# Moving side work of a two-layer S5, retention and convolution trunk: sums at other gate blocks, k0 ahead of the last state-space output, low parts among the value products, one operand place fewer

## The chip, the cores and the metric

The kernel runs on one core of a Trainium2 chip. The metric is the device time of one execution in microseconds (us). Engine names are those of the profile: PE is TensorE (matmuls), PEld its weight loads, DVE is VectorE, ACT is ScalarE, POOL is GpSimd, SP is SyncE, which here issues every DMA from one queue in order (SPq).

## What is computed

A trunk of two layers on x of shape (1, 1024, 1024), each `x = x + mixer(rmsnorm(x))`, then a final norm. Layer 0's mixer, cut to what matters here:

```python
u_s5, g_s5, q, k, v, g_ret = jnp.split(h @ w_in, cuts, axis=-1)
y_s5 = s5_mixer(u_s5, ...)            # diagonal state space, gelu, GLU
y_s5 = y_s5 * jax.nn.silu(g_s5)
y_ret = retention(q, k, v) * jax.nn.silu(g_ret)   # 8 heads, rotary q and k
return jnp.concatenate([y_s5, y_ret], axis=-1) @ w_out
```

Layer 1 is a convolution module: an input projection into a, b and a gate, a width-31 depthwise convolution, a layer norm and an output projection.

## The kernel before, in words

Matrices lie transposed: features on the 128 partitions, the 1024 tokens in two halves of 512. Every large product is done with operands split into a high part and a low part (`wh`, `wl` for weights, `xh`, `xl` for x), and three matmuls per block of 128 (high x high, high x low, low x high; L269 to L271, `mm3`). A `gemm` is 24 matmuls of 128x512 for one half, so a projection block of 128 features takes 48. Weights come by DMA as `wf` (512 KB), ACT casts the high part `wh`, and DVE or POOL subtracts to get the low part `wl`. `wnext` hands them out in the order that `plan` laid down.

`layer0_front` makes x's parts, then blocks u0 to u7 (input of the state-space layer), then gate blocks g8 to g23, 48 matmuls each. Between the gate blocks stand the steps of the state-space layer for B = 0 to 7, two gate blocks each: `s5_tables` (POOL), `s5_states`, and `s5_out(B - 1)`. `s5_states` writes a kernel Kt to DRAM (`k_d`, L876), reads it back as a banded tile `Wd` (L879), and ACT copies it to `W1` (L881). `s5_out` runs 16 matmuls of W1 and U (L896) and 32 of W3 and S (L902) into two banks y0 and y1, ACT copies these to `yb` (L906), and a DMA stores `yb` in `y_d` (L908). `s5_out(7)` comes last, behind g23.

Three helpers make sums for Strassen-Winograd products and put them in DRAM, and are called inside the loop over the gate blocks, on tiles with the tags wa to wd, two of each. `input_sums` (4 calls) loads four quarters of x (256 KB each), scales and adds on ACT and DVE, and stores four sums `xt1` to `xt4`. `weight_sums` (8 calls) does the same for the output weights on DVE (`a`, `ws`, L237 to L247); `value_sums` (4 calls, POOL) for the value weights (`va`, `vs`). The calls for x stand behind gate blocks 9, 11, 13 and 15, those for the output weights behind blocks 16 to 23.

`retention` works by four pairs of heads. For each pair `ret_proj` projects k and q (48 matmuls each), DVE takes them out of PSUM as `kraw` and `qraw` (L970), four DMAs swap their halves (`kswp`, `qswp`, L979), POOL multiplies by the rotary tables (L983, L985) and DVE adds (`krot`, `qrot`, L986). In pair 0 `ret_values` follows: the value projection as seven products of half size (order 1, 2, 6, 7, 3, 4, 5; 48 matmuls each), whose x operands are four tile pairs each. Products 1, 2 and 3 use quarters of x itself; 6, 7, 4 and 5 use the sums xt2, xt3, xt4 and xt1, which `fetch` loads and splits into two places of 8 tiles. DVE and ACT then add the products and scale them per token into `v` (L1019). `ret_heads` transposes k (`ktp`, L1062), decays it (`kt`, L1064), makes state updates (`kv`, L1081; `S`, L1091), scores (`sp`, L1098; `sc`, L1104) and outputs (`ro`, L1125 and L1130), normalises them and multiplies by the gate. Each pair also makes two `y_pass` steps for the state-space branch: a load of `yp` from `y_d` (L915), gelu on ACT (`yn`, L917, with a table load), and a store to `yn_d` (L918).

`weight_low` prepares low parts of layer 1's input weights: a load `lf` of 256 KB (L224), a cast `lh` on ACT (L225), a subtraction on DVE (L226), a store `lo` (L229). `LOWS` = 16 of 32 are made in pairs 1 and 2, behind the second mask of that pair, on tiles with one buffer each; the rest in the GLU loop of `layer0_back_and_layer1`.

The order on each engine is set by a scheduler from the program's order, its own estimates of times, the pools' free buffers, and `issue_after`, which keeps what stands inside it from being issued before a named instruction. Each engine then runs its list in order. PSUM has 3 banks for projections (`ps_mm`) and 5 for the rest (`ps_aux`).

Of the kernel before, what the change touches and what calls it, by code (L numbers as in the profile page):

```python
# [19 lines left out]
P = 128  # L20
# [3 lines left out]
HALF = 512  # L24
# [32 lines left out]
class Trunk:  # L57
# [272 lines left out]
    def layer0_front(self, st):  # L330
# [3 lines left out]
        early = ExitStack()  # L334
# [585 lines left out]
    def retention(self, st):  # L920
        nc, A = self.nc, self.A
        r0 = self.r0 = self.pool("ret0", 1, stack=st)
        early = ExitStack()
        rq = self.rq = self.pool("retq", 1, stack=early, side="right")
        self.vt = [[(r0 if d else rq).tile([P, 4, HALF], F32, name=f"v{d}_{h}") for h in range(2)] for d in range(2)]
        self.rk = rq.tile([P, 2, T], F32, name="ropek")
        nc.sync.dma_start(self.rk[:], A["rope_k"])
        self.mask = r0.tile([P, NH, P], F32, name="retmask")
        nc.sync.dma_start(self.mask[:], A["ret_mask"])
        self.g128 = r0.tile([P, 4], F32, name="g128")  # L930
        nc.sync.dma_start(self.g128[:], A["ret_g128"])
        self.reps = r0.tile([P, NH], F32, name="reteps")
        nc.sync.dma_start(self.reps[:], A["ret_eps"])
        for pair in range(4):
            cur = list(self.ret_proj(pair))[-1]
            if pair == 0:
                with ExitStack() as vst:
                    V = self.ret_values(self.pool("vp", 1, stack=vst))
                self.rp = self.pool("ret", 1, stack=st)
                self.kdec = self.rp.tile([P, NH, 64], F32, name="kdec")  # L940
                nc.sync.dma_start(self.kdec[:], A["ret_kdec"])
                ry = self.pool("rety", 1, stack=early, side="right")
            with ExitStack() as held:
                if pair:
                    held.enter_context(self.tc.issue_after(self.last_rs.ins))
                for cb in (2 * pair, 2 * pair + 1):
                    self.y_pass(ry, cb)

            def turned():
                if pair == 3:  # L950
                    early.close()
                    self.lp = self.pool("l1", side="right")
            if pair in (1, 2):
                with self.tc.issue_after(self.masked[1].ins):
                    for k in range(LOWS // 2 * (pair - 1), LOWS // 2 * pair):
                        self.weight_low(ry, k, (("wa", "wb"), ("wc", "wd")), 1)
            self.ret_heads(pair, *cur, V, turned)

    def ret_proj(self, pair):
        nc, A, rp = self.nc, self.A, self.r0  # L960
        raws = {}

        def project(nm):
            w = self.wnext(f"{nm}{pair}")
            raw = raws[nm] = self.rq.tile([P, T], F32, name=f"{nm}raw_{pair}", tag="raw", bufs=2)
            for h in range(2):
                c = slice(h * HALF, (h + 1) * HALF)
                ps = self.bank(f"mm_{nm}{pair}_{h}", aux=False)
                self.gemm(ps[:], w, self.xs[h])
                last = nc.vector.tensor_tensor(raw[:, c], ps[:], self.R[:, c], op=ALU.mult)  # L970
            return last

        def turn(nm, behind=None):
            raw, tab = raws[nm], self.rk
            swp = self.rq.tile([P, T], F32, name=f"{nm}swp_{pair}", tag="swp", bufs=2)
            o = rp.tile([P, T], F32, name=f"{nm}rot_{pair}", tag=f"{nm}rot", bufs=1)
            for b in range(4):
                s = b ^ 1
                nc.sync.dma_start(swp[32 * b:32 * b + 32, :], raw[32 * s:32 * s + 32, :])  # L979
            cs = [slice(h * HALF, (h + 1) * HALF) for h in range(2)]  # L980

            for c in cs:
                nc.gpsimd.tensor_tensor(o[:, c], raw[:, c], tab[:, 0, c], op=ALU.mult)  # L983
            for c in cs:
                nc.gpsimd.tensor_tensor(swp[:, c], swp[:, c], tab[:, 1, c], op=ALU.mult)  # L985
            return o, [lambda c=c: nc.vector.tensor_tensor(o[:, c], o[:, c], swp[:, c], op=ALU.add) for c in cs]  # L986


        project("k")
        yield None  # L990
        krot, adds = turn("k")
        last = project("q")
        with self.tc.issue_after(last.ins):
            for add in adds:
                add()
        qrot, qadds = turn("q")
        if pair % 2 == 0:
            for add in qadds:
                add()
            qadds = ()  # L1000
        yield krot, qrot, qadds

    def ret_values(self, vp):
# [1 line left out]
        nc, v = self.nc, self.nc.vector  # L1005
        vt = self.vt

        def fetch(i, slot):
            res = []
            for kb in range(4):  # L1010
                a, b = (vp.tile([P, HALF], F32R, name=f"xt{i}{q}{kb}", tag=f"xt{slot}", bufs=8) for q in "hl")
                nc.sync.dma_start(b[:].bitcast(F32), self.xt_d[i][kb])
                nc.scalar.copy(a[:], b[:].bitcast(F32))
                v.tensor_tensor(b[:], b[:].bitcast(F32), a[:].bitcast(F32), op=ALU.subtract)
                res.append((a, b))
            return res
# [4 lines left out]
        xs = {1: self.xs[0][:4], 2: self.xs[0][4:], 3: self.xs[1][4:]}  # L1021
        m, u3 = ([vp.tile([P, HALF], F32, name=f"{n}{b}") for b in range(4)] for n in ("vm", "vu"))
        for n, i in enumerate(V_ORDER):
            if i in (1, 2):
                xs[i + 5] = fetch((2, 3)[i - 1], i)
            pss = [self.bank(f"mm_v{i}_{b}", aux=n % 2 == 0 or b == 3) for b in range(4)]
            for j in range(2):
                wh, wl = (t[:].rearrange("p (k a) n -> p k (a n)", a=4) for t in self.wnext(f"V{i}_{j}"))
                for b in range(4):
                    o = slice(b * P, (b + 1) * P)  # L1030
                    for k in range(2):
                        xh, xl = xs[i][2 * j + k]
                        first, last = j == k == 0, j == k == 1
                        nc.tensor.matmul(pss[b][:], xh[:, o], wh[:, k, :], start=first, stop=False)  # L1034
                        nc.tensor.matmul(pss[b][:], xh[:, o], wl[:, k, :], start=False, stop=False)  # L1035
                        nc.tensor.matmul(pss[b][:], xl[:, o], wh[:, k, :], start=False, stop=last)  # L1036
            if i in (6, 7):
                xs[{6: 4, 7: 5}[i]] = fetch({6: 4, 7: 1}[i], i - 5)
            for b, ps in enumerate(pss):
                if i == 1:  # L1040
                    nc.scalar.copy(m[b][:], ps[:])
                elif i in (2, 4):
                    v.tensor_tensor(ps[:], ps[:], (m if i == 2 else u3)[b][:], op=ALU.add)
                    scaled(i // 4, 0, b, ps[:])
                else:
                    v.tensor_tensor((u3 if i == 7 else m)[b][:], ps[:], m[b][:], op=ALU.add)
                    if i == 5:
                        scaled(0, 1, b, m[b][:])
                        v.tensor_tensor(ps[:], ps[:], u3[b][:], op=ALU.add)
                        scaled(1, 1, b, ps[:])  # L1050
# [686 lines left out]
```

## Time and profile before

| | us |
|---|---|
| median of 3 runs | 1213.87 (1213.17 to 1214.84) |
| the profiled execution | 1213.96 |
| its span | 1212.2 |
| outside the span | 1.8 |
| mean granted TensorE clock | 0.989 |

The profile is of one execution on the one core. Busy time counts an engine's instructions, not its waits. A timeline row gives the start in us from the span's start, the time, the engine, the line, the operation with the tiles it writes and reads, the shapes, and the number of instructions joined; behind it in brackets stands how long the engine had been idle and what ended that. A clock of 1.00 is TensorE's full speed. The DMA share is the mean busy share of the core's 16 DMA engines.

### The profile page before, as it was taken

The numbers are of one execution on the slowest core, as the hardware profiler recorded it, in microseconds if no ns is written. First come the engines' busy times: TensorE is split into PE (matmuls) and PEld (weight loads), VectorE is DVE, ScalarE is ACT, GpSimd is POOL, SyncE is SP. The second block draws the span as 40 slices with busy tenths as digits, with TensorE's granted clock in tenths as the row PEclk, the third lists the DMA queues.
The fourth block names the chain that finished last, engine by engine and source line by source line (L and its number), as shares of the span: only waits on it lengthen the run. The fifth ranks groups of instructions, "written<-read, shape, count | busy, mean of one in ns | idle before, by whom it ended". The sixth has DMA issues, their size and how long they took to land.

```text
span 1212.2 us, 17495 instructions
## 1 busy us (share of the span) xinstructions
PE 1173.8 (97%) x6150; PEld 972.0 (80%) x6150; DVE 920.3 (76%) x1525; ACT 550.4 (45%) x827; POOL 681.7 (56%) x489
## 2 busy tenths in 40 slices
PE   8999999999979999799899999999999999999997
PEld 7888888888868888678688888878887888788877
DVE  6966866899436537688788979469999999999643
ACT  7222333332124354234444645267765668444662
POOL 2059987788813233423344132518896578987642
PEclk9999999999989999899999999999999999999999
DMA  9362556587797546875898657865547653356863
GB/s 334 105 200 81 195 203 215 195 284 278 261 354 254 166 147 212 282 246 189 333 333 291 223 208 241 286 254 198 174 148 267 248 190 117 126 187 230 276 245 138
DMA packets 130904, 270.14 MB, mean 223 GB/s; under 512 B 12800, under 2 KB 41728, under 8 KB 130688
## 3 DMA queue, kind: packets, MB, share of 16 engines
q1 hardware_dynamic: 130816, 269.02, 65.2%
q8 instruction: 48, 0.79, 0.3%
q14 instruction: 40, 0.33, 0.1%
HBM read 193.02 MB, written 71.76 MB: 218 GB/s over the span
## 4 chain that ended last, share of the span: by engine, by line
PE 77%; DMA 8%; DVE 7%; POOL 2%; issue 2%; ACT 2%; SPq 1%; DVEq 0%; POOLq 0%; ACTq 0%
PE mm_g L271 6%; PE mm_g L270 6%; PE mm_g L269 6%; PE mm_w L269 4%; PE mm_w L270 4%; PE mm_w L271 3%; PE mm_u L271 2%; PE mm_u L270 2%; PE mm_oc L271 2%; PE mm_oc L269 2%; PE mm_oc L270 2%; PE mm_u L269 2%; PE mm_v L1036 2%; PE mm_v L1034 2%; PE mm_v L1035 2%
## 5 line engine op out<-in xcount | busy, mean ns | idle before, releaser
L1426 DVE SCALAR_TENSOR_TENSOR cv<-u,convw,cv 128x512 f32<-128x512 f32 x358 | 245.3, 748 | 5.7 <-ACT cv L1412 3.9
L1406 POOL TENSOR_TENSOR tp<-tp,tp 128x512 f32<-128x512 f32 x104 | 138.9, 1339 | 33.0 <-ACT tp L1405 27.3
L271 PE MATMUL mm_g<-xh,wl_g 128*128 128x512 f32 x256 | 100.8, 394 | 0.0
L270 PE MATMUL mm_g<-xl,wh_g 128*128 128x512 f32 x256 | 100.6, 393 | 0.0
L269 PE MATMUL mm_g<-xh,wh_g 128*128 128x512 f32 x256 | 100.4, 392 | 0.0
L1405 ACT ACTIVATE tp<-u,convw 128x512 f32<-128x512 f32 x104 | 69.3, 714 | 9.2 <-POOL tp L1406 9.0
L270 PEld LDWEIGHTS mm_g<-xl,wh_g 128*128 128x128 f32 x256 | 48.1, 188 | 11.3 <-issue 1.6
L271 PEld LDWEIGHTS mm_g<-xh,wl_g 128*128 128x128 f32 x256 | 48.0, 188 | 10.5
L269 PEld LDWEIGHTS mm_g<-xh,wh_g 128*128 128x128 f32 x256 | 48.1, 188 | 9.6
L271 PE MATMUL mm_oc<-zh,wl_woc 128*128 128x512 f32 (+1 forms) x152 | 54.7, 360 | 0.7 <-DMA wl_woc<-lo_woc 0.7
L269 PE MATMUL mm_oc<-zh,wh_woc 128*128 128x512 f32 (+1 forms) x152 | 54.5, 362 | 0.0
L270 PE MATMUL mm_oc<-zl,wh_woc 128*128 128x512 f32 (+1 forms) x152 | 54.2, 356 | 0.0
L271 PE MATMUL mm_g<-h1h,wl_cg 128*128 128x512 f32 x128 | 50.0, 390 | 1.1 <-POOL wl_cg L261 1.1
L270 PE MATMUL mm_u<-xl,wh_u 128*128 128x512 f32 x128 | 49.9, 390 | 0.9 <-DVE xl L383 0.9
L270 PE MATMUL mm_b<-h1l,wh_cb 128*128 128x512 f32 x128 | 50.5, 394 | 0.3 <-DVE h1l L1343 0.3
L270 PE MATMUL mm_glu<-yl,wh_glu 128*128 128x512 f32 x128 | 50.5, 395 | 0.2 <-DVE yl L1165 0.2
L269 PE MATMUL mm_glu<-yh,wh_glu 128*128 128x512 f32 x128 | 50.6, 397 | 0.0
L269 PE MATMUL mm_u<-xh,wh_u 128*128 128x512 f32 x128 | 49.4, 396 | 1.2 <-ACT wh_u L260 1.1
L271 PE MATMUL mm_glu<-yh,wl_glu 128*128 128x512 f32 x128 | 50.4, 394 | 0.0
L269 PE MATMUL mm_g<-h1h,wh_cg 128*128 128x512 f32 x128 | 50.3, 393 | 0.0
L271 PE MATMUL mm_a<-h1h,wl_ca 128*128 128x512 f32 x128 | 50.3, 393 | 0.0
L269 PE MATMUL mm_b<-h1h,wh_cb 128*128 128x512 f32 x128 | 49.9, 390 | 0.4 <-ACT h1h L1342 0.4
(833 smaller groups left out, 3607.7 us busy)
## 6 DMA issues: line engine op xcount, KB each, us to landing
wf_g<-w_ab SPq DMA_DIRECT2D x16, 512.0 KB, 4.6
a<-w_out SPq DMA_DIRECT2D x32, 256.0 KB, 4.5
ws<-a SPq DMA_DIRECT2D x32, 256.0 KB, 4.9
lf<-w_c SPq DMA_DIRECT2D x32, 256.0 KB, 5.1
wf_p<-ws SPq DMA_DIRECT2D x16, 512.0 KB, 3.8
wf_cb<-w_c SPq DMA_DIRECT2D x16, 512.0 KB, 4.8
wf_ca<-w_c SPq DMA_DIRECT2D x16, 512.0 KB, 4.8
wl_cb<-lo_cb SPq DMA_DIRECT2D x16, 512.0 KB, 3.4
```

What stands on the lines that cost most here:

```text
L269: nc.tensor.matmul(ps, wh[:, kb, :], xh, start=start, stop=False)
L270: nc.tensor.matmul(ps, wh[:, kb, :], xl, start=False, stop=False)
L271: self.last_mm = nc.tensor.matmul(ps, wl[:, kb, :], xh, start=False, stop=stop)
L1034: nc.tensor.matmul(pss[b][:], xh[:, o], wh[:, k, :], start=first, stop=False)
L1035: nc.tensor.matmul(pss[b][:], xh[:, o], wl[:, k, :], start=False, stop=False)
L1036: nc.tensor.matmul(pss[b][:], xl[:, o], wh[:, k, :], start=False, stop=last)
L1405: nc.scalar.mul(sk[:], u[:, k:k + HALF], cw[:, nb, k:k + 1])
L1406: gp.tensor_tensor(s0[:], s0[:], sk[:], op=ALU.add)
L1426: v.scalar_tensor_tensor(dst[:], *tap, accs_[i][:], op0=ALU.mult, op1=ALU.add)
```

## The change

1. `LOWS` goes from 16 to 18.
2. The calls of `input_sums` stand behind gate blocks 9, 10, 11 and 12, those of `weight_sums` behind 13 to 20.
3. k0's two gemms are issued at the end of `layer0_front`, ahead of `s5_out(7)`; their banks are kept, and `ret_proj` takes them from there.
4. The calls of `weight_low` leave pairs 1 and 2. `ret_values` makes three behind the last sum of each product from the second on, on the tags wa to wd with two buffers.
5. `ret_values` has one operand place of 8 tiles fewer. xt2 and later xt4 are split into the four tile pairs of x's first quarter of the second token half (`x12`), which no product reads; during product 5 that quarter is loaded again from `xT`, scaled and split. Loads go through staging tiles `xf` on the tags wa and wc.
6. The sums of the products are regrouped: product 1 and the sums of 7 and 3 are scaled on ACT as they come; 2, 4 and 5 are added with one scalar_tensor_tensor per target on DVE.

```diff
-LOWS = 16
+LOWS = 18
...
-                if nb >= 16:
-                    self.weight_sums(sums, nb - 16)
-                elif nb % 2:
-                    self.input_sums(sums, (nb - 8) // 2)
+                if 9 <= nb < 13:
+                    self.input_sums(sums, nb - 9)
+                elif 13 <= nb < 21:
+                    self.weight_sums(sums, nb - 13)
+        w, self.k0 = self.wnext("k0"), [self.bank(f"mm_k0_{h}", aux=False) for h in range(2)]
+        for h in range(2):
+            self.gemm(self.k0[h][:], w, xs[h])
         self.s5_out(7)
...
-            if pair in (1, 2):
-                with self.tc.issue_after(self.masked[1].ins):
-                    for k in range(LOWS // 2 * (pair - 1), LOWS // 2 * pair):
-                        self.weight_low(ry, k, (("wa", "wb"), ("wc", "wd")), 1)
...
-                ps = self.bank(f"mm_{nm}{pair}_{h}", aux=False)
-                self.gemm(ps[:], w, self.xs[h])
+                ps = self.k0[h] if early else self.bank(f"mm_{nm}{pair}_{h}", aux=False)
+                if not early:
+                    self.gemm(ps[:], w, self.xs[h])
...
+        def fetch(i, tiles):
+            for kb, (a, b) in enumerate(tiles):
+                g = self.vec(V_NG0, kb)
+                f = vp.tile([P, HALF], F32, name=f"xf{i}{kb}", tag=("wa", "wc")[kb % 2], bufs=2)
+                nc.sync.dma_start(f[:], self.xt_d[i][kb] if i else self.A["xT"][kb, :, HALF:])
+                if i:
+                    nc.scalar.copy(a[:], f[:])
+                    v.tensor_tensor(b[:], f[:], a[:].bitcast(F32), op=ALU.subtract)
+                else:
+                    nc.scalar.mul(a[:], f[:], g)
+                    v.scalar_tensor_tensor(b[:], f[:], g, a[:].bitcast(F32), op0=ALU.mult, op1=ALU.subtract)
+            return tiles
...
+        def summed(d, h, b, ps):
+            o, r = vt[d][h][:, b, :], self.Rtok[:, 4 * h + b:4 * h + b + 1]
+            self.last_sum = v.scalar_tensor_tensor(o, ps, r, o, op0=ALU.mult, op1=ALU.add)
+
+        x12 = self.xs[1][:4]
+        spare = [tuple(vp.tile([P, HALF], F32R, name=f"xt{q}{kb}") for q in "hl") for kb in range(4)]
+        xs = {1: self.xs[0][:4], 2: self.xs[0][4:], 3: self.xs[1][4:], 6: fetch(2, x12), 7: fetch(3, spare)}
...
             if i in (6, 7):
-                xs[{6: 4, 7: 5}[i]] = fetch({6: 4, 7: 1}[i], i - 5)
+                xs[{6: 4, 7: 5}[i]] = fetch(*{6: (4, x12), 7: (1, spare)}[i])
+            if i == 4:
+                fetch(0, x12)
             for b, ps in enumerate(pss):
                 if i == 1:
                     nc.scalar.copy(m[b][:], ps[:])
+                    scaled(0, 0, b, ps[:])
                 elif i in (2, 4):
-                    v.tensor_tensor(ps[:], ps[:], (m if i == 2 else u3)[b][:], op=ALU.add)
-                    scaled(i // 4, 0, b, ps[:])
+                    summed(i // 4, 0, b, ps[:])
+                elif i == 5:
+                    summed(0, 1, b, ps[:])
+                    summed(1, 1, b, ps[:])
                 else:
...
+                    t = (u3 if i == 7 else m)[b]
+                    self.last_sum = v.tensor_tensor(t[:], ps[:], m[b][:], op=ALU.add)
+                    for d, h in {6: (), 7: ((1, 0), (1, 1)), 3: ((0, 1),)}[i]:
+                        scaled(d, h, b, t[:])
+            with self.tc.issue_after(self.last_sum.ins) if n > 1 else nullcontext():
+                for k in range(LOWS * (n - 1) // 6, LOWS * n // 6) if n else ():
+                    self.weight_low(vp, k, (("wa", "wb"), ("wc", "wd")), 2)
```

More of the change, by code (lines that the diff above doesn't have):

```diff
@@ L963, in project @@
         def project(nm):
-            w = self.wnext(f"{nm}{pair}")
+            early = nm == "k" and pair == 0
+            w = None if early else self.wnext(f"{nm}{pair}")
             raw = raws[nm] = self.rq.tile([P, T], F32, name=f"{nm}raw_{pair}", tag="raw", bufs=2)
@@ L1006, in ret_values @@
         vt = self.vt
[L1008 to L1016, printed above, removed]
+        def fetch(i, tiles):
[10 more added lines that the diff above has]
+            return tiles
         def scaled(d, h, b, src):
             nc.scalar.mul(vt[d][h][:, b, :], src, self.Rtok[:, 4 * h + b:4 * h + b + 1])
-        xs = {1: self.xs[0][:4], 2: self.xs[0][4:], 3: self.xs[1][4:]}
+        def summed(d, h, b, ps):
[4 more added lines that the diff above has]
+        xs = {1: self.xs[0][:4], 2: self.xs[0][4:], 3: self.xs[1][4:], 6: fetch(2, x12), 7: fetch(3, spare)}
         m, u3 = ([vp.tile([P, HALF], F32, name=f"{n}{b}") for b in range(4)] for n in ("vm", "vu"))
         for n, i in enumerate(V_ORDER):
-            if i in (1, 2):
-                xs[i + 5] = fetch((2, 3)[i - 1], i)
             pss = [self.bank(f"mm_v{i}_{b}", aux=n % 2 == 0 or b == 3) for b in range(4)]
@@ L1041, in ret_values @@
                     nc.scalar.copy(m[b][:], ps[:])
+                    scaled(0, 0, b, ps[:])
                 elif i in (2, 4):
-                    v.tensor_tensor(ps[:], ps[:], (m if i == 2 else u3)[b][:], op=ALU.add)
-                    scaled(i // 4, 0, b, ps[:])
-                else:
[L1046 to L1050, printed above, removed]
+                    summed(i // 4, 0, b, ps[:])
+                elif i == 5:
+                    summed(0, 1, b, ps[:])
+                    summed(1, 1, b, ps[:])
+                else:
+                    t = (u3 if i == 7 else m)[b]
[5 more added lines that the diff above has]
+                    self.weight_low(vp, k, (("wa", "wb"), ("wc", "wd")), 2)
         return lambda p, b, hh: vt[p // 2][b // 4][:, b % 4, (2 * (p % 2) + hh) * P:(2 * (p % 2) + hh + 1) * P]
```

## The prediction

> **What bounds the kernel now.** I read the page's busy times first, then what PE waited for, then busy time by stage, then the timeline around each stall.
>
> The page, part 1:
>
> ```profile
> PE 1173.8 (97%) x6150; PEld 972.0 (80%) x6150; DVE 920.3 (76%) x1525; ACT 550.4 (45%) x827; POOL 681.7 (56%) x489
> ```
>
> PE is busy for 1173.8 of the span's 1212.2 us, so an edit off PE is worth only what it does to the 38.4 us in which PE stands still or to the clock beside them. PE's waits (engine, line, releaser: us in all, times, longest):
>
> ```profile
> PE y L896 <- ACT W L881: 7.8, 1, 7.8
> PE sp L1098 <- DVE qrot L986: 6.4, 3, 3.8
> PE kv L1081 <- DVE kt L1064: 2.9, 1, 2.9
> PE ktp L1062 <- DVE krot L986: 2.7, 2, 1.6
> ...
> PE ro L1125 <- DVE sc L1104: 1.4, 1, 1.4
> ```
>
> These five are 21.2 us, all in the stretch that the change edits. Stage by stage (from:to, length, busy us of PE, PEld, DVE, ACT, POOL, granted clock, DMA share, GB/s):
>
> ```profile
> 233.00:320.00 87.00, 87.00 (x593) 72.67 (x591) 74.19 (x82) 25.61 (x45) 78.77 (x56) 1.00 0.78 272
> 333.50:346.40 12.90, 5.07 (x28) 4.49 (x28) 2.77 (x5) 3.58 (x5) 4.05 (x4) 0.60 1.01 326
> 346.40:447.00 100.60, 100.60 (x459) 82.35 (x456) 55.10 (x69) 36.63 (x51) 26.51 (x14) 1.00 0.63 209
> 491.80:507.00 15.20, 8.50 (x58) 7.12 (x58) 10.53 (x20) 1.68 (x3) 2.48 (x2) 0.78 0.96 328
> 507.00:537.50 30.50, 27.76 (x172) 23.28 (x171) 26.27 (x72) 13.31 (x17) 14.29 (x9) 0.94 0.69 216
> 567.00:586.00 19.00, 16.12 (x102) 12.80 (x101) 10.17 (x17) 6.26 (x8) 2.66 (x3) 0.91 0.72 240
> ```
>
> Row 1 is the second half of the gate blocks with the weight sums: DVE and POOL are busy for 85% and more, yet PE never stops. Row 2 is the stall ahead of y_7. Row 3 holds k0, q0 and the values: no PE idle, full clock. Rows 4 to 6 are the retention's pairs 1, 2 and 3: 6.70, 2.74 and 2.88 us idle. Every row with a stall also shows a clock below 1, so a stall costs more than its length.
>
> **The change, part by part.**
>
> *k0's gemm ahead of s5_out(7).* PE's timeline (start, us, operation, count, wait), the last gate matmuls, y_7 and an undisturbed y:
>
> ```profile
> 289.76 1.95 PE L896 MATMUL y<-U,W 128*128 128x128 f32 x16
> 291.64 2.06 PE L902 MATMUL y<-S,W 64*128 64x128 f32 x32
> ...
> 325.76 0.39 PE L270 MATMUL mm_g<-xl,wh_g 128*128 128x512 f32 x1
> ...
> 333.46 0.39 PE L271 MATMUL mm_g<-xh,wl_g 128*128 128x512 f32 x1
> 341.68 3.78 PE L896 MATMUL y<-U,W 128*128 128x128 f32 x16 [7.83 <-ACT W L881]
> 345.40 2.47 PE L902 MATMUL y<-S,W 64*128 64x128 f32 x32
> ```
>
> The undisturbed y runs from 289.76 to 293.70, 3.94 us; y_7 takes 6.19 us (341.68 to 347.87). So the stall costs 7.83 + 2.25 = 10.1 us. What ended it, on ACT and SP:
>
> ```profile
> 333.62 0.98 SPq L879 DMA_DIRECT2D Wd<-k_d  x1
> 340.59 1.04 ACT L881 COPY W<-Wd 128x1024 f32<-128x1024 f32 x1 [16.86 <-DMA Wd<-k_d]
> ```
>
> From the gate rows, 34 matmuls take 7.70 us, 0.2265 each; k0's 48 take 10.9 us, from 333.7 to 344.6. W is ready at 341.64, so y_7 starts 2.9 us after it could, and both the wait and the slow clock go: **-10.1 us**. W should rather come earlier, because the weight sums' loads and stores that make the DMA share 1.01 in that window are gone from it.
>
> What is late next: k0's evacuation, which DVE runs in order, now waits for y_7's store (its tile takes that place). y_7 ends at 348.6, the two copies at about 349.6; the store lands as a row of the DMA list says:
>
> ```profile
> y_d<-yb SPq DMA_DIRECT2D x8, 512.0 KB, 4.1
> ...
> lf<-w_c SPq DMA_DIRECT2D x32, 256.0 KB, 5.1
> ```
>
> So k0's evacuation ends near 355. q0's second half takes k0's first bank; PE gets there after q0's first 24 matmuls and 15 of value product 1, some 39 x 0.2265 = 8.8 us behind y_7, near 357.4: no stall. Behind it on DVE stand qraw, four splits of x2's sums, the krot additions (their swap DMAs wait for kraw) and then wl_V2_0, which PE needs near 371. I count it ready between 369.5 and 373, so 0 to 2.5 us, and take **+1.0**.
>
> *Sums at other gate blocks.* Weight sums move from blocks 16-23 to 13-20; row 1 shows such blocks without a stall. Input sums move from every second block to 9-12 in a row, where ACT waits for their loads:
>
> ```profile
> ACT xa L206 <- DMA xa<-xT: 19.4, 3, 9.1
> ```
>
> Two of these multiplications now stand on ACT ahead of a block's W2 copy, which PE needs about 22 matmuls (5 us) after the transposes. Bounds 0 (cover holds) and 4.1 (a 9.1 us wait less 5); I take 0, because PE never waited for them before.
>
> *Low parts inside the values, one operand place fewer.* 18 loads, 18 ACT casts, 18 DVE subtractions and 18 stores of 256 KB enter row 3, with 4 restoring loads, casts and STTs; weight-sum traffic leaves it. DVE has 45 us free there, ACT 64. PE does no more; what counts is order. Each wh cast and wl subtraction must end before its half product starts:
>
> ```profile
> 402.94 1.05 ACT L164 CAST wh_V<-wf_V 128x1024 fp32r<-128x1024 f32 x1 [0.16 <-PE mm_v L1036]
> ...
> 404.07 2.85 POOL L165 TENSOR_TENSOR wl_V<-wf_V,wh_V 128x1024 fp32r<-128x1024 f32 x1 [6.86 <-ACT wh_V L164]
> ```
>
> A low's cast ahead of wh_V in ACT's order can wait a landing of 5.1 us. Following SP's, ACT's and DVE's new orders through the products with those rows, wh_V4_0 is the tightest, 1 to 2 us ahead of need; the rest have 4 or more. I take 0, bounds 0 and 5. The x2-to-x4 rewrite of one place has a whole product of 10.9 us between its last reader and next user; the fewer sums on DVE and more scalings on ACT have no PE reader until pair 0.
>
> *No low parts in pairs 1 and 2.* Pair 1 before, in order of time:
>
> ```profile
> 478.92 2.08 ACT L917 ACTIVATE yn<-yp 128x1024 f32<-128x1024 f32 x1
> 482.86 0.67 DVE L970 TENSOR_TENSOR qraw<-mm_q,R 128x512 f32<-128x512 f32 x1
> 486.31 2.04 ACT L917 ACTIVATE yn<-yp 128x1024 f32<-128x1024 f32 x1 [5.31 <-DMA yp<-y_d]
> 488.38 0.33 SPq L918 DMA_DIRECT2D yn_d<-yn  x1
> 489.37 2.41 POOL L261 TENSOR_TENSOR wl_k<-wf_k,wh_k 128x1024 fp32r<-128x1024 f32 x1 [3.48 <-ACT wh_k L260]
> 489.45 2.74 SPq L979 DMA_DIRECT2D qswp<-qraw  x4
> 489.85 2.48 DVE L226 TENSOR_TENSOR lh<-lf,lh 128x512 fp32r<-128x512 f32 x1 [5.11 <-ACT lh L225]
> 494.04 1.27 DVE L1064 TENSOR_TENSOR kt<-ktp,kdec 128x512 f32<-128x512 f32 x2
> 494.77 1.75 PE L1081 MATMUL kv<-v,kt 128*64 128x128 f32 x28 [2.94 <-DVE kt L1064]
> 497.10 2.48 POOL L985 TENSOR_TENSOR qswp<-qswp,ropek 128x512 f32<-128x512 f32 x2 [5.33 <-DMA qswp<-qraw]
> 500.28 2.47 PE L1098 MATMUL sp<-qrot,krot 64*128 64x128 f32 x18 [3.76 <-DVE qrot L986]
> ```
>
> DVE stood 5.11 us for a low's cast, which stood behind gelu (486.31), and kt came after two lows: that is kv's 2.9. The q swap stood on SP behind a gelu store: that is sp's 3.8. Row 4's clock of 0.78 over 15.20 us is 3.3 us at most; I take 3.0. Together 6.7 + 3.0 = 9.7. After, no low stands in either queue, k1's gemm comes wholly ahead of pair 0's heads, so its swap leaves early, and between the k and q swaps SP holds two gelu stores, the later of them for the activation that ended at 481.0 before and, with the heads 15 matmuls later, near 482 or 483 now. The q swap then leaves with its source (qraw, 483.5), 6 us earlier than at 489.45. From that issue to sp passed 10.8 us, so the q side is ready at 494.3. With kv's wait gone, kv runs from 491.8 to 493.6, and 3 matmuls of k2 more stand ahead of it: PE asks for sp at 494.3. I leave 0.5 for what slips. **-9.2 us**; at worst (only kt's wait gone) -4.
>
> Pair 2: ktp's 2.7 and a clock of 0.94 over 30.5 us (1.8 at most; I take 1.5) go, since krot no longer stands behind lows: -4.2. But SP now holds two gelu stores and a gelu load ahead of the q swap. That is pair 3's order before:
>
> ```profile
> 551.25 2.05 PE L1130 MATMUL ro<-v,sc 128*128 128x128 f32 x16
> 566.95 2.08 ACT L917 ACTIVATE yn<-yp 128x1024 f32<-128x1024 f32 x1 [4.94 <-DMA yp<-y_d]
> 569.05 0.32 SPq L918 DMA_DIRECT2D yn_d<-yn  x1
> 569.41 2.83 SPq L979 DMA_DIRECT2D qswp<-qraw  x4
> ```
>
> There the swap left 16.1 us after the last ro ended, and sp waited 2.65 us in two pieces (6.4 less 3.8). Pair 2 inherits 1 to 5 us, clock included; I take +3.5. Net **-0.7**. Pair 3 keeps its order: 0. The GLU loop loses two lows of 16; none of the five waits lies behind pair 3: 0.
>
> [...] Rows 5 and 6 show the clock at 0.94 and 0.91 though no single wait there exceeds 1.6 us. [...]
> DVE's low took 2.48 us beside POOL's wl_k (489.37), where qraw, as large but with one input in PSUM, took 0.67 (482.86). [...]
>
> **Sum.** -10.1 + 1.0 - 9.2 - 0.7 = -19.0. The profiled execution took 1213.96 us (span 1212.2 and 1.8 around it), 0.09 over the median, which I neglect: 1213.96 - 19.0 = **1195**.
>
> **Rivals.**
> A. The forecast, 1191 to 1200: 0.48.
> B. Pair 1's q swap still waits: its gelu store slips, sp waits its 3.8 and the clock falls, kt is held too. The -9.2 is lost: 1204. For it: SP's order still has gelu stores ahead of the swap. Against: no low in between. 0.17.
> C. The front of the values or the input sums stall PE: two stalls of about 2.5 us with 1.5 of clock each, 8 us: 1203. For it: the 0 to 2.5 above. 0.10.
> D. Slower: the low loads in the values. Each low's load waits for its place, its cast waits for the load in front of the next wh_V, SP holds the next weight load behind a low's store. If six products each lose 5.1 us of landing less 1.8 of slack, plus 1.7 of clock (between the 1.5 and 2.25 above), that is 6 x 5.0 = 30 on top of 1195: 1225. It decides from 3.6 us lost in each product (21.4 in all). For it: pair 1 shows just this chain. Against: row 3's free time and the 4 us I find for most products. 0.13.
> E. No effect: W comes later than k0's end, and the swaps wait as before: 1214. 0.04.
> F. Better: pair 2's stall vanishes, no loss in the values: 1191 or below. 0.08.
>
> The measurement can tell about 0.2% (2.4 us). Faster: A, B, C, F = 0.83; same 0.04; slower 0.13. A range of 1189 to 1207 holds A, B, C and most of F, and leaves out D and E.
>
> **What would show it.** Right: no wait of y for W, y at about 3.9 us; clock 1.00 from 320 to the pairs; kt and sp of pair 1 without waits over 1 us; sp of pair 2 waiting 1 to 3 us for qrot. Wrong: PE's waits naming wl_V, wh_V or a value operand; a wait of v or kp matmuls for ACT near blocks 10 to 12; sp of pair 1 still waiting 3 us or more.

## Result and profile after

The changed kernel takes 1204.83 us (median; 1202.50 to 1211.58), the kernel before beside it 1213.39: ratio **0.9941 [0.9919, 0.9963]**, faster by 0.6%. The forecast was 1195, so the time lies in the upper half of the range given, and the saving, 7 us by the ratio and 8.6 by the medians, is less than half of the 19 us forecast. The profiled execution's span went from 1212.2 to 1202.9 us.

PE's waits in the changed kernel (engine, line, releaser: us in all, times, longest):

```profile
PE sp L1113 <- DVE qrot L987: 8.0, 4, 5.0
PE ro L1140 <- DVE sc L1119: 3.0, 2, 2.8
PE mm_w L271 <- DVE wl_p L165: 1.8, 1, 1.8
```

The wait of y for W is gone, and so are that of ktp and kv's 2.9 us in pair 1 (0.7 us of a kv wait stand in pair 0). What stands there instead is later: sp (of which 5.0 in one piece, in pair 2), ro, and the first matmuls of w_out's stage (mm_w). Busy time by stretch, same columns as in the prediction:

```profile
334.30:349.20 14.90, 14.90 (x98) 12.75 (x98) 3.14 (x3) 5.17 (x7) 3.54 (x3) 1.00 0.91 298
349.20:436.90 87.70, 87.70 (x384) 72.09 (x385) 61.82 (x73) 47.78 (x73) 25.46 (x14) 1.00 0.76 258
463.00:496.00 33.00, 32.51 (x232) 27.45 (x231) 26.35 (x87) 11.38 (x13) 18.40 (x12) 1.00 0.70 206
517.80:530.00 12.20, 7.17 (x58) 5.89 (x57) 5.94 (x12) 0.40 (x1) 2.48 (x2) 0.72 0.51 173
559.30:584.00 24.70, 17.74 (x140) 14.36 (x141) 17.05 (x38) 7.71 (x12) 7.46 (x5) 0.93 0.89 333
```

Rows 1 and 2 are k0 with y_7 and then q0 with the values: PE full, clock 1.00. Row 3 is pair 1, 0.49 us idle in 33.0, where before had 6.70 in the 15.2 of its stall. Rows 4 and 5 are the end of pair 2 and pair 3: 5.03 and 6.96 us idle, clock 0.72 and 0.93.

To put a price on each stage I use one measure in all profiles: for every PE instruction the distance from its start to the next one's, less the median distance that instructions writing the same tile have in the changed kernel, added up by stage. One set of medians serves all versions, because sp's own median lies at 56 ns in one version and at 104 in another. A pair's stage ends with its last ro. The measure counts waits and slow clock together; a negative figure means slightly better than the median.

| TensorE loss, us | before | after | difference | forecast |
|---|---|---|---|---|
| y_7 to end of values | 10.54 | -0.47 | -11.0 | -10.1 + 1.0 |
| pair 0 | 0.02 | 0.77 | +0.7 | 0 |
| pair 1 | 9.98 | 1.00 | -9.0 | -9.2 |
| pair 2 | 4.75 | 7.06 | +2.3 | -0.7 |
| pair 3 | 7.76 | 10.70 | +2.9 | 0 |
| rest of the GLU | 0.85 | 0.09 | -0.8 | 0 |
| w_out's stage | 3.79 | 6.83 | +3.0 | 0 |
| layer 1's blocks | 2.33 | 3.92 | +1.6 | 0 |

By the end of pair 1 the changed kernel is about 19 us ahead, as forecast (18.3); behind that it loses 9 of them. The rows add up to 10.1 us, the spans differ by 9.3: the stretches ahead of y_7 and behind layer 1's blocks are not in the table. The question of the experiments is whether this is chance, or whether the stages behind take back by a mechanism, and by which.

### The profile page after: what moved, and what is told of

Read it like the earlier page. It is cut to its first block, busy times and chain, and to the rows that moved or that the text cites. A ratio compares the mean times of both kernels' runs of the same rounds, so it can differ in the third digit from the quotient of the medians.

```text
span 1202.9 us, 17525 instructions
## 1 busy us (share of the span) xinstructions
PE 1173.1 (98%) x6150; PEld 972.4 (81%) x6150; DVE 938.3 (78%) x1529; ACT 551.5 (46%) x831; POOL 688.5 (57%) x489
## 4 chain that ended last, share of the span: by engine, by line
PE 77%; DMA 8%; DVE 8%; issue 2%; POOL 2%; ACT 2%; SPq 1%; DVEq 0%; POOLq 0%; ACTq 0%
PE mm_g L271 7%; PE mm_g L270 7%; PE mm_g L269 6%; PE mm_w L269 4%; PE mm_w L270 4%; PE mm_w L271 4%; PE mm_oc L269 2%; PE mm_oc L270 2%; PE mm_oc L271 2%; PE mm_u L271 2%; PE mm_u L270 2%; PE mm_u L269 2%; PE mm_b L270 2%; PE mm_b L271 2%; PE mm_a L270 2%
## 5 line engine op out<-in xcount | busy, mean ns | idle before, releaser
L270 PE MATMUL mm_g<-h1l,wh_cg 128*128 128x512 f32 x128 | 50.5, 394 | 0.0
L269 PE MATMUL mm_a<-h1h,wh_ca 128*128 128x512 f32 x128 | 50.1, 392 | 0.0
```

The source lines that it names most:

```text
L269: nc.tensor.matmul(ps, wh[:, kb, :], xh, start=start, stop=False)
L270: nc.tensor.matmul(ps, wh[:, kb, :], xl, start=False, stop=False)
```

## Experiments

All ratios are against the kernel before, run beside each version in the same series; "before" lay at 1210.7 to 1212.1 us there. Single runs of one kernel scatter by 7 to 12 us where there are eight or more, so times are read with their intervals, and stages by the measure above. Each stage figure is of one execution: e9's edit does not touch the first stage, and yet it loses 1.8 us less there than before, so a difference of less than 2 us in one stage of one profile proves little by itself.

| TensorE loss, us | y_7..values | pair 1 | pair 2 | pair 3 | w_out | span |
|---|---|---|---|---|---|---|
| before | 10.54 | 9.98 | 4.75 | 7.76 | 3.79 | 1212.2 |
| after | -0.47 | 1.00 | 7.06 | 10.70 | 6.83 | 1202.9 |
| e2: k0 back | 6.82 | 3.98 | 6.44 | 10.53 | 6.27 | 1208.0 |
| e7: k0 alone | 9.14 | 8.50 | 2.76 | 8.45 | 4.33 | 1207.7 |
| e10: k0 and sums alone | 0.28 | 9.88 | 4.14 | 5.10 | 3.91 | 1198.1 |
| e3: low parts back in pairs | 0.88 | 11.99 | 4.19 | 8.75 | 3.59 | 1204.0 |
| e1: q swaps first | -0.47 | 2.17 | 4.99 | 7.30 | 9.32 | 1197.8 |
| e5: e1, GELU DMAs on ACT | -0.36 | 6.83 | 0.19 | 4.06 | 3.36 | 1189.6 |
| e11: same, from pair 2 on | 0.26 | 3.16 | 0.19 | 5.31 | 4.25 | 1190.2 |
| e12: e5, low parts in pairs | 0.22 | 0.98 | 7.34 | 11.22 | 2.93 | 1198.9 |
| e9: before, cure of e5 | 8.73 | 8.31 | 6.20 | 3.23 | 2.91 | 1205.8 |
| e4: GLU's lows held | -0.47 | 1.72 | 7.72 | 5.78 | 8.29 | 1202.3 |
| e6: split of w_out first | -0.44 | 1.48 | 7.13 | 11.15 | 3.71 | 1199.1 |
| e8: e5 and e6 | -0.47 | 5.11 | 0.21 | 4.85 | 2.23 | 1189.5 |

### What took the wait for W: k0, or the sums?

**e2, k0 back** behind s5_out(7), the rest as changed:

```diff
-        w, self.k0 = self.wnext("k0"), [self.bank(f"mm_k0_{h}", aux=False) for h in range(2)]
-        for h in range(2):
-            self.gemm(self.k0[h][:], w, xs[h])
         self.s5_out(7)
...
-            early = nm == "k" and pair == 0
+            early = False
```

> The changed kernel with k0's gemm back behind s5_out(7); sums, low parts and operand places as changed. Theory of the prediction (the term of 10.1 us is k0's cover): y_7 waits again. But W was ready at 338.6 in the changed kernel against 341.6 before, 4.2 us behind the last gate matmul, so of the 10.1 only some 6 us come back (4.2 of wait, 1.5 to 2 of clock): 1210 to 1211. Rival 1 (sums of later blocks were not what delayed W): wait of 7 to 8 us, time 1214. Rival 2 (k0's move costs elsewhere what it saves): time within 2 us of 1204.8.

Measured: 1210.32, 0.9994 [0.9971, 1.0017], as the theory had it. y waits for W again:

```profile
PE y L896 <- ACT W L881: 5.5, 1, 5.5
```

Without k0's move the rest of the change is worth nothing that the time shows.

**e7, k0 alone** on the kernel before (the first three lines that the diff above removes, added to it, and `early` as in the change):

> The kernel before with the k0 projection's matmuls moved ahead of the last s5_out and nothing else; sums, low parts and value operands as before. This tells apart the parts of the 11.0 us that TensorE's loss from y_7 to the end of the values fell by. Forecast's step (48 matmuls, 10.9 us, cover the 9.9 us wait for W whole): loss in that stage 10.5 us to about 0.5, end of values 10 us earlier; W itself is no earlier. Rival (W's own lateness counts too, and the sums' move bought the rest): about 7.3 us of the loss go, some 3 us of y wait stay. In the later stages the forecast's rule (nothing changes behind) gives 1202 to 1204; if what is gained at y_7 is given back later, 1206 to 1210.

Measured: 1211.39, 1.0006 [0.9989, 1.0024]; the theory's 10 us did not come. y's wait is gone, as the theory has it (the rival kept 3 us of it), but a wait almost as long stands behind it. PE's longest wait, then rows of ACT, SP and DVE of this version:

```profile
PE mm_q L269 <- DVE kraw L975: 6.3, 1, 6.3
```

```profile
348.79 1.07 ACT L909 COPY yb<-y 128x512 f32<-128x512 f32 x2 [1.98 <-issue]
```

```profile
358.19 2.84 SPq L247 DMA_DIRECT2D ws<-a  x4
361.37 0.32 SPq L911 DMA_DIRECT2D y_d<-yb  x1
```

```profile
359.52 0.68 DVE L245 TENSOR_TENSOR a<-a,a 128x512 f32<-128x512 f32 x1
367.66 0.69 DVE L975 TENSOR_TENSOR kraw<-mm_k,R 128x512 f32<-128x512 f32 x1 [7.45 <-DMA y_d<-yb]
```

y_7's copies end at 349.86, but its store leaves SP only at 361.37, behind the weight sums' stores, which wait for DVE's additions (the last at 359.52). kraw takes the place of the store's source and starts when the store has landed, at 367.66, and q0's second half needs k0's bank. From the end of the copies the store stood 11.5 us on SP. In the changed kernel no weight sum is left by then:

```profile
350.34 0.33 SPq L911 DMA_DIRECT2D y_d<-yb  x1
```

```profile
353.70 1.29 DVE L971 TENSOR_TENSOR kraw<-mm_k,R 128x512 f32<-128x512 f32 x2 [6.17 <-DMA y_d<-yb]
```

**e10, k0 and the sums' new blocks**, nothing else, on the kernel before (k0's lines as in e7):

```diff
-                if nb >= 16:
-                    self.weight_sums(sums, nb - 16)
-                elif nb % 2:
-                    self.input_sums(sums, (nb - 8) // 2)
+                if 9 <= nb < 13:
+                    self.input_sums(sums, nb - 9)
+                elif 13 <= nb < 21:
+                    self.weight_sums(sums, nb - 13)
```

> The kernel before with two parts of the change alone: the k0 matmuls ahead of the last s5_out, and the sums at the changed kernel's gate blocks. Low parts and the operands of the values as before. k0 alone took 1.4 us off the loss of 10.5 us from y_7 to the end of the values, everything but k0 took 3.7. Theory (k0's matmuls cover the wait for W only if the y_d store that frees kraw's memory is not queued on SP behind the weight sums' stores, so both are needed): loss in that stage under 0.5 us, end of values about 10 us earlier than before. Rival (the operands in front of the values have a part in it, by the y_d store or by the order on SP): 2 to 6 us of loss stay. Time, by what the stages behind did in the other runs: 1203 to 1206 for the theory, 1207 to 1211 for the rival.

Measured: 1203.21, 0.9913 [0.9880, 0.9945]; loss 0.28 in that stage. The theory holds: k0 alone takes 1.4 us off the 10.5 (no more than the scatter), both together 10.3. And these two parts alone give as much as the whole change (0.9941): the intervals overlap, so the low parts' move and the fewer operand place add nothing that shows in the time. The stage shows 0.7 us for the operand place: a value product takes 10.88 us on x's own tiles and 11.24 on the tiles made for the sums, at clock 1.00 in both, and the changed kernel has two of the second kind where e10 has four. Why the tiles differ was not looked into.

### Where the low parts' gain went

**e3**, the 18 low parts back in pairs 1 and 2, the rest as changed:

```diff
+            if pair in (1, 2):
+                with self.tc.issue_after(self.masked[1].ins):
+                    for k in range(LOWS // 2 * (pair - 1), LOWS // 2 * pair):
+                        self.weight_low(ry, k, (("wa", "wb"), ("wc", "wd")), 1)
...
-            with self.tc.issue_after(self.last_sum.ins) if n > 1 else nullcontext():
-                for k in range(LOWS * (n - 1) // 6, LOWS * n // 6) if n else ():
-                    self.weight_low(vp, k, (("wa", "wb"), ("wc", "wd")), 2)
```

> The changed kernel with the 18 low parts back in pairs 1 and 2, nine each, behind the second mask and with one buffer; the values hold none. Theory (low parts in DVE's, ACT's and SP's queues set pair 1's waits): kv and sp of pair 1 wait again, 5 to 7 us with 3 us of clock, pair 2 shows ktp waits of 2 to 4 us in place of the 5 us of sp; time 1210 to 1215. Rival (pair 1 was freed by k1's gemm and its swap coming ahead of pair 0's heads, not by the lows leaving): pair 1's waits stay under 1.5 us and the time stays near 1205.

Measured: 1203.66, 0.9935 [0.9912, 0.9958], as fast as the changed kernel. Pair 1 loses 11.0 us more, about what the theory has, though by waits of rt and sp and not of kv; pairs 2 and 3 and w_out's stage lose 2.9, 1.9 and 3.2 less, 8.0 in all. So in these queues the low parts cost pair 1 what the forecast said, and their going is paid back behind it for the most part.

### The mechanism behind: q's swap on SP

After's pair 2 on SP, then on POOL, then on PE:

```profile
510.36 0.33 SPq L921 DMA_DIRECT2D yn_d<-yn  x1
510.79 0.38 SPq L918 DMA_DIRECT2D yp<-y_d  x1
511.26 2.26 SPq L980 DMA_DIRECT2D qswp<-qraw  x3
513.62 1.02 SPq L1174 DMA_DIRECT2D yr_d<-grl  x2
514.69 1.32 SPq L980 DMA_DIRECT2D qswp<-qraw  x1
```

```profile
521.38 2.48 POOL L986 TENSOR_TENSOR qswp<-qswp,ropek 128x512 f32<-128x512 f32 x2 [7.63 <-DMA qswp<-qraw]
```

```profile
524.55 2.47 PE L1113 MATMUL sp<-qrot,krot 64*128 64x128 f32 x18 [5.04 <-DVE qrot L987]
526.95 0.79 PE L270 MATMUL mm_k<-xl,wh_k 128*128 128x512 f32 x1
```

The swap is four DMAs. The first three leave SP right behind a GELU's store and the next GELU's load, the fourth only behind two yr_d stores. POOL gets the rotated half at 521.38, PE waits 5.04, and the three matmuls behind take 0.6 to 0.8 us instead of 0.39.

**e1**, a pair's yr_d stores held until the next pair's last swap has left:

```diff
-        for hh in range(2):
-            h = 2 * pair + hh
-            nc.sync.dma_start(self.yr_d[h * P:(h + 1) * P], gts[hh][:])
+        self.kept = [(2 * pair + hh, gts[hh]) for hh in range(2)]
...
+    def gate_stores(self, held=True):
+        with self.tc.issue_after(self.last_swap.ins) if held else nullcontext():
+            for h, gt in self.__dict__.pop('kept', ()):
+                self.nc.sync.dma_start(self.yr_d[h * P:(h + 1) * P], gt[:])
```

> The changed kernel with the two yr_d stores of each pair's gate products held until the next pair's last q swap DMA is issued; all else alike, and SP's order differs in pair 2 only by the fourth qswp_2 piece, which now stands directly behind the third. Theory (pair 2's 5.04 us wait of sp is the fourth piece standing 3.4 us later on SP, behind two 512 KB stores): POOL's qswp_2 starts 4 us earlier and sp of pair 2 waits 0 to 1.5 us; the last ro of pair 2 comes 5 to 7 us earlier with the clock, and the time falls to about 1199, if pair 3 does not take it back. Rival (the wait is set by the two gelu stores ahead of the first piece, which leave at 510.4): sp still waits 4 us or more, and the time stays within 1 us of 1204.8.

Measured: 1203.11, 0.9933 [0.9913, 0.9953]. POOL starts at 518.58, 2.8 us earlier, and sp of pair 2 no longer waits, but now kt's second half stands on DVE behind q's rotation and kv waits 3.0:

```profile
519.88 1.74 DVE L987 TENSOR_TENSOR qrot<-qrot,qswp 128x512 f32<-128x512 f32 x1 [6.15 <-POOL qswp L986]
521.54 0.68 DVE L1079 TENSOR_TENSOR kt<-ktp,kdec 128x512 f32<-128x512 f32 x1
```

Pair 2 loses 5.0 instead of 7.1, and w_out's stage 2.5 more. Half right: the fourth piece was late by those stores, but the first three, behind the GELU's store, were late too.

**e5**, in addition the GELU pass's DMAs on ACT's queue:

```diff
-        nc.sync.dma_start(yt[:], self.y_d[cb].rearrange("i h g m -> (h g) i m"))
+        nc.scalar.dma_start(yt[:], self.y_d[cb].rearrange("i h g m -> (h g) i m"))
...
-        nc.sync.dma_start(self.yn_d[cb * P:(cb + 1) * P], yn[:].rearrange("p m i -> p (m i)"))
+        nc.scalar.dma_start(self.yn_d[cb * P:(cb + 1) * P], yn[:].rearrange("p m i -> p (m i)"))
```

> The version with the yr_d stores held, and in addition the GELU pass's yp load and yn_d store issued on ACT's queue instead of SP's, so that in pairs 1 to 3 no store that waits for a GELU stands ahead of a q swap on SP. Theory (the remaining stalls of pairs 1 to 3 are the q swap's head of line on SP): q's rotated copy comes at least 2 us earlier, kt's second half is in front of it on DVE again, the kv wait of 3.0 us of the version with the stores held goes; TensorE's loss in pair 2 falls from 5.0 us to 1 to 2, the sp waits of pair 3 (2.5 us) go; layer time 1197 to 1200. Rival 1 (the swap's own landing and POOL's work set it, or the issues on ACT delay ACT's copies): pair 2 stays at 4 to 6 us, 1202 to 1205. Rival 2 (what is won in the pairs comes back as waits for weight splits): pair losses fall by 4 to 6 us and the loss of the w stage rises by as much, 1202 to 1204.

Measured: 1191.95, **0.9857 [0.9830, 0.9885]**, better than the theory's range. Pair 2 on DVE and PE:

```profile
518.85 1.36 DVE L1079 TENSOR_TENSOR kt<-ktp,kdec 128x512 f32<-128x512 f32 x2 [1.47 <-PE ktp L1077]
521.00 1.77 DVE L987 TENSOR_TENSOR qrot<-qrot,qswp 128x512 f32<-128x512 f32 x1 [0.79 <-POOL qswp L986]
```

```profile
523.98 1.75 PE L1097 MATMUL kv<-v,kt 128*64 128x128 f32 x28
525.66 1.38 PE L1114 MATMUL sp<-qrot,krot 64*128 64x128 f32 x18
```

kt is in front of q's rotation again, and neither kv nor sp waits: pair 2's loss is 0.19. The w_out stage, which this edit doesn't touch, falls to 3.36. But pair 1 rose to 6.83, so that pairs 1 and 2 together lose 7.0 where the changed kernel lost 8.1: what the profile gains lies in pair 3 (6.6 us less), w_out's stage (3.5 less) and layer 1 (1.6 less, see the end). Why w_out's stall goes too was not followed up. ACT in pair 1, first in the changed kernel, then in this version:

```profile
460.62 1.99 ACT L920 ACTIVATE yn<-yp 128x1024 f32<-128x1024 f32 x1 [4.33 <-DMA yp<-y_d]
462.62 1.28 ACT L540 ACT_TABLE_LOAD   x1
```

```profile
463.90 2.07 ACT L920 ACTIVATE yn<-yp 128x1024 f32<-128x1024 f32 x1 [2.75 <-DMA yp<-y_d]
466.36 1.28 ACT L540 ACT_TABLE_LOAD   x1 [0.39 <-ACT yn L920]
```

The GELU ends 3.4 us later, the rs behind it 3.7, and through DVE the q swap leaves at 478.49 instead of 474.74.

**e11**, therefore, moves only the GELU passes of pairs 2 and 3:

```diff
+        (nc.scalar if cb >= 4 else nc.sync).dma_start(yt[:], self.y_d[cb].rearrange("i h g m -> (h g) i m"))
```

and the yn_d store likewise.

> The version with the stores held and the GELU pass on ACT's queue, but only for the GELU passes of pairs 2 and 3; those of pairs 0 and 1 on SP as in the changed kernel. In the version with all of them on ACT's queue pair 1 lost 6.9 us (the changed kernel: 1.0), as the yp load waited on ACT behind its casts, the GELU's end and with it the table load for rs came 3.7 us later, and rs sets turn, transposes and the q swap. Theory: pair 1's loss goes back to 1 to 2 us, pair 2 stays at 0.2 to 1, pair 3 at about 4; time 1186 to 1189. Rival (pair 2's good state came from pair 1 running later, or the stages behind take it back): pair 2 or the w stage loses 4 to 6 us again, 1191 to 1195.

Measured: 1190.62, **0.9805 [0.9774, 0.9837]**, the lowest ratio, though its interval overlaps e5's and the two spans are alike (1190.2 and 1189.6); the theory had 1186 to 1189. Pair 1's loss is halved (3.16, not the 1 to 2 expected), pair 2 stays at 0.19. So pair 2 does not owe its state to e5's late pair 1, except for at most the 2.2 us by which pair 1 is still later than in the changed kernel. PE's waits of this version, then 440 to 590 us in after and in this version:

```profile
PE sp L1114 <- DVE qrot L987: 1.5, 1, 1.5
PE kv L1097 <- DVE kt L1079: 1.5, 2, 1.1
PE mm_glu L269 <- ACT yh L1184: 1.4, 1, 1.4
```

```profile
440.00:590.00 150.00, 136.83 (x918) 114.55 (x917) 107.64 (x312) 53.11 (x61) 53.89 (x34) 0.97 0.71 227
```

```profile
440.00:590.00 150.00, 144.43 (x971) 121.15 (x971) 114.23 (x328) 58.43 (x69) 57.00 (x36) 0.99 0.75 239
```

The same stretch holds 53 matmuls more and 7.6 us less idle.

### Does the cure need the change, and the change the cure?

**e9**, the cure of e5 on the kernel before (the diffs of e1 and e5):

> The kernel before with the queue cure alone (the yr_d stores of a pair held behind the next pair's last q swap; the GELU pass's yp loads and yn_d stores on ACT's queue). Tells whether the cure's 12 us belong to the changed kernel or to any version. Theory (in before the low parts of w_out and the GELU stores both stand in front of the q swap; the cure takes only the second): TensorE's loss falls in pair 3 from 7.1 to about 4 us and in pair 2 from 4.1 to about 2, in pair 1 (9.4) little; time 4 to 7 us below before, so that the change is worth 11 to 15 us on top of the cure. Rival (the cure is worth the same 12 us without the change): about 12 us below before, and the change is worth 6 to 7 us on top as it is without the cure. Second rival (the low parts on DVE set it all): within 2 us of before.

Measured: 1208.66, 0.9969 [0.9945, 0.9994], 3.5 us, just under the theory's 4 to 7. Pair 3 lost 3.23, somewhat less than the 4 expected; pair 2, expected at 2, lost 6.20, more than before. With the queue cured on both sides, the change is worth 0.9857 / 0.9969 = 0.9888, 13.5 us, against 7 to 9 without (the two ratios are of different series); by the two profiles' spans 16.2.

**e12**, e5 with the low parts back in pairs 1 and 2 (the diff of e3):

> The version with the stores held and all GELU passes on ACT's queue (1192), with the 18 low parts of w_out back in pairs 1 and 2, nine each, as in the run of the low parts alone, where this cost pair 1 10.5 us and the whole nothing. Theory (the low parts' move is worth its forecast 9 us when the stages behind don't give it back): pair 1 loses 8 to 12 us more than its counterpart or pair 2 does, time 1199 to 1203. Rival (the later stages absorb it again): 1191 to 1195, with less loss in pair 3 and in the w stage.

Measured: 1199.71, 0.9882 [0.9854, 0.9910]; e11, in the same series, 1190.62; e5, in another, 0.9857, with a span 9.3 us shorter than here. The time is in the theory's range, but the ratios of e5 and e12 differ by 3 us with overlapping intervals, and the spans by 9. The stages were not those expected: pair 1 lost 0.98, pairs 2 and 3 some 7 more each than in e5, with this wait the longest, in pair 3:

```profile
PE mm_glu L269 <- ACT yh L1185: 7.6, 1, 7.6
```

So nine low parts in pair 1 cost it nothing here, while e9, also with low parts in pair 1 and the GELU's DMAs on ACT, loses 8.31 there. Low parts in the queues are not enough for pair 1's stall; what else it takes is open.

### The two smaller stalls

**e4**: in pair 3 the mask multiplication (sc) that ro waits for stood on DVE behind a low part of the GLU loop:

```profile
576.72 1.81 DVE L226 TENSOR_TENSOR lh<-lf,lh 128x512 fp32r<-128x512 f32 x1 [1.97 <-ACT lh L225]
578.46 1.27 DVE L1119 TENSOR_TENSOR sc<-sp,retmask 128x512 f32<-128x512 f32 x2
```

The low parts of the GLU loop held behind the mask:

```diff
+              with self.tc.issue_after(self.masked[1].ins):
```

> The changed kernel with the low parts of the GLU loop held until pair 3's second score mask is issued; PE's order stays but for three matmuls. Theory (ro of pair 3 waits 2.77 us for sc, because a low's subtraction, itself waiting for its cast and load, stands ahead of the mask on DVE): that wait falls under 1 us, and the time by 2 to 3 us. Rival (the mask itself is late because sp and the kv sums are late): the wait stays near 2.8.

Measured: 1203.55, 0.9922 [0.9898, 0.9945]. ro's wait goes, as the theory has it and against the rival, and pair 3 loses 4.9 less; but rt waits 2.4 and mm_w 4.8 in three pieces, and from pair 0 to the end of w_out's stage 26.3 us are lost, in the changed kernel 26.4. The 2 to 3 us did not come.

**e6**: after's DVE at the start of w_out's stage, and PE behind it:

```profile
663.16 0.69 DVE L1299 TENSOR_TENSOR yr0g<-yr0g,t2f 128x512 f32<-128x512 f32 x1
664.57 1.58 DVE L1299 TENSOR_TENSOR yr0g<-yr0g,t2f 128x512 f32<-128x512 f32 x2 [0.72 <-DMA yr0g<-yr_d]
666.08 1.21 DVE L165 TENSOR_TENSOR wl_p<-wf_p,wh_p 128x1024 fp32r<-128x1024 f32 x1
```

```profile
667.34 0.50 PE L271 MATMUL mm_w<-ysh,wl_p 128*128 128x512 f32 x1 [1.78 <-DVE wl_p L165]
...
669.63 0.63 PE L269 MATMUL mm_w<-ysh,wh_p 128*128 128x512 f32 x1
```

One more yr0g stands ahead of these, at 661.95. In before the split came second in this row (676.23, one yr0g ahead of it) and nothing waited. The subtractions behind the split (`split11` is the subtraction that writes wl_p1_1):

```diff
+                        with self.tc.issue_after(self.split11.ins):
+                            v.tensor_tensor(f[:], f[:], t2f[kb][:], op=ALU.subtract)
```

> The changed kernel with one difference: the four yr0g subtractions (L1299) stand behind the split wl_p1_1 (L165) on DVE instead of ahead of it. Theory (the 1.8 us wait for wl_p1_1 at 667 us and the half clock behind it come from those subtractions in front of the split): that wait goes, the w stage's loss falls from 6.8 us to about 3.8 (before's 3.8), time about 3 us less, 1201 to 1202. Rival (ACT's half of the split, or the next split, is late by itself, so another mm_w wait takes its place): loss stays at 6 to 7 us, 1204 to 1205.

Measured: 1201.44, 0.9931 [0.9910, 0.9952]; the stage's loss falls to 3.71, the 3.1 us expected, and no other wait takes its place there. The time does not settle it: the ratio is 0.001 lower than the changed kernel's, well inside both intervals.

**e8**, e5 and e6 together (the diffs of e1, e5 and e6):

> Both remedies together: yr_d stores held, the GELU pass's DMAs on ACT's queue, and wl_p1_1 ahead of the yr0g subtractions. Theory (each stall has a place of its own): the gains add, pair 2 at 1 to 2 us, w stage at 4 us, 1194 to 1198. Rival (the stages behind take back what is won ahead of them): 1200 to 1203.

Measured: 1193.66, 0.9870 [0.9838, 0.9901], no better than e5: its w_out stage had lost that stall already (3.36; here 2.23).

## Why the forecast was right and wrong

**y_7 and k0: right in size, wrong in one cause.** The step forecast -10.1 + 1.0, the stage gave -11.0: the 10.1 went, the 1.0 did not come (k0's evacuation ended at 354.99, near the 355 forecast, and no product waited), and 0.7 came from the value products' faster operand tiles, which the forecast did not have. But it put all of the 10.1 down to k0's 48 matmuls and set the sums' move at 0 (bounds 0 to 4.1). k0's move alone does 1.4 (e7), everything but k0 3.7 (e2). The forecast had said that k0's evacuation waits for y_7's store; it did not ask what would stand ahead of that store on SP if the sums stayed. The sums' move is worth 8.9 us on top of k0's (e7 to e10). That W itself would come earlier fits; after's ACT:

```profile
337.52 1.05 ACT L884 COPY W<-Wd 128x1024 f32<-128x1024 f32 x1 [13.18 <-DMA Wd<-k_d]
```

W is there at 338.6, in before at 341.6; with the sums where before has them it came at 340.1 (e7) and 339.4 (e9), so part of the 3 us is scatter.

**Low parts in the values: right.** No product waited; rivals C and D, a stall at the values' front and a slow chain of lows, didn't happen.

**Pair 1: right in size, its cause in part open.** -9.2 forecast, -9.0 found; kv waits for nothing there, sp 0.45 us, and e3 brings 11.0 us back. But e12 has low parts in pair 1 too and loses 0.98, so they do not set that stall alone. Rival B's 1204 fits the time but not the place: q's swap waited, a pair later.

**Pair 2: the step that failed first.** "Pair 2 inherits 1 to 5 us, clock included; I take +3.5." The stage lost 7.06; net +2.3 in place of -0.7. The mechanism, GELU stores in front of the swap, was the one named, but it was sized by pair 3's swap, which left in one piece; here the fourth piece stood behind the yr_d stores as well. e1 and e5 show both parts: 2.1 us by the first, 4.8 more by the second, of which e11 leaves at most 2.2 to a later pair 1.

**Pair 3, "keeps its order: 0", and the GLU loop and w_out, 0: the terms that were missing.** They came to +2.9 and +3.0. The order in the program is the same, but in the trace other instructions stand in front: pair 2's last ro ends 16 us earlier than before, and not everything beside it moves by as much. A low came in front of the mask in pair 3, three more subtractions in front of a split in w_out's stage. e6 shows the second; for the first, e4 removes the wait but not the loss, so its whole cause stays open. That stages take back is shown from several sides: e3 gives 11.0 us of pair 1 away and gets 8.0 back, e10 gets the whole gain with half the change, and e5 and e11 save 17 and 24 us of before's time by their ratios once SP is clear. Some 4 of e5's are the cure's own (e9); e11's placement was not tried on before.

**Layer 1, +1.6: not the change.** In all 14 profiles r_ps waits 1.2 us there; in 8 the blocks lose 2.3 us, in 6 they lose 3.9, in versions of either kind. Pair 0's +0.7 is one wait of kv for kt, 0.68 us.

**The clock.** The forecast went by the rows and let short waits cost clock; that holds: behind the 1.78 us wait above, matmuls took 0.63 us at a granted clock of 0.50 (668.4 to 671.6 us), where the last ones ahead of it took 0.39.

## What to carry to other kernels

Here a gain in one stage was kept only where the queues behind it could run earlier too. Before adding a gain up, go through each in-order queue (SP above all) and ask which store that waits for something stands ahead of a transfer on PE's path (in e7 the y_d store stood 11.5 us on SP). Size such a wait by all its DMAs, the last piece included, and give stages that "keep their order" a price too when what is ahead of them moves by several us. Two edits that show no gain without each other (e7, e2) can be worth 9 to 10 us together (e10), when one leaves a wait almost as long as the one it removes.

## Of the hardware, not expected

The same wait costs clock in one execution and not in another. Before and after in layer 1, PE's rows of r_ps and of one matmul behind it:

```profile
923.01 2.00 PE L532 MATMUL r_ps<-ones,s1q 128*128 128x64 f32 x16 [1.20 <-POOL s1q L504]
...
925.60 0.40 PE L269 MATMUL mm_g<-h1h,wh_cg 128*128 128x512 f32 x1
```

```profile
911.97 2.00 PE L535 MATMUL r_ps<-ones,s1q 128*128 128x64 f32 x16 [1.24 <-POOL s1q L507]
...
914.88 0.63 PE L269 MATMUL mm_g<-h1h,wh_cg 128*128 128x512 f32 x1
```

1.20 and 1.24 us of waiting, and matmuls of 0.40 and 0.63 us behind them, at a granted clock of 1.00 (924.8 to 927.8 us of before) and 0.50 (914.2 to 917.3 us of after). What decides between the two was not shown. The length of the wait does not sort the profiles: 1.20 to 1.24 us in the 8 that lose 2.3 us in layer 1's blocks, 1.19 to 1.24 in the 6 that lose 3.9. This short stall thus had two prices, its length or its length and some 1.6 us.
